# Transposing q and k of the first attention branch by VectorE and a DRAM tile, normalising x^T one section earlier, and re-timing the pre-added weight sums

## The chip, the cores and the metric

One core of a Trainium2 chip runs the whole program. The metric is the device time in microseconds of one execution; lower is better. The profiled execution that the rows come from is one such run, with its own time. Engines are named as in the profile: PE is TensorE (matmuls), DVE is VectorE, ACT is ScalarE, POOL is GpSimd, SP is SyncE, and a q behind a name is that engine's own DMA queue.

## What is computed

A decoder layer on 512 tokens of width 1024, in fp32, with two attention branches of 8 heads of 64 side by side. Cut to what matters:

```python
h = rms_norm(x, norm_w)
proj = h @ w_in
qa, ka, va, za, qb, kb, vb, zb, gl_a, gl_b = split(proj)
qa = rms_norm(split_heads(qa, 8), q_norm_w)
ka = rms_norm(split_heads(ka, 8), k_norm_w)
oa = moba_attention(qa, ka, va, rel_bias)   # at this length: causal softmax with a relative bias
ob = stick_breaking_attention(qb, kb, vb)
ya = (merge_heads(oa) * silu(za)) @ w_up_moba
yb = (merge_heads(ob) * silu(zb)) @ w_up_sb
y = sigmoid(gl_a + gb[:1024]) * ya + sigmoid(gl_b + gb[1024:]) * yb
return x + y @ w_out
```

## The kernel before

Every fp32 matmul is done as three matmuls on a high and a low part (`mm3`, lines 170 to 174): each weight chunk of 128x1024 is loaded by SP's queue as `wr` (line 124), ScalarE makes its high part `wh` (line 133) and VectorE the difference `wl` (line 135). `load_w` keeps three chunks ahead. SP, ScalarE and VectorE thus each do one step per chunk, and a chunk feeds 24 matmuls in the first part of the kernel.

Four sections come first (`section_tc`, called at lines 222, 328, 340, 347). Each computes one of qa, ka, va, vb, with tokens on the partitions, in four chunks of weights; after chunk c it calls `hooks[c]`, which is how the work on the result of the section before is put between. In the first section x^T is loaded as `xr` beside the first four weight chunks (`raw_x`, `fetch_w`) and split unnormalised. The row norms `r` are computed at the end of it (`row_norm`), and a copy `R` along the free dimension is fetched through DRAM (lines 230, 231).

qa and ka are normalised by head: ScalarE squares, VectorE sums, GpSimd makes the factors (`head_norm`), and VectorE multiplies the rows (`head_rows`, tiles `qan`, `kan`). Then TensorE transposes them, 16 blocks of 128x128 each, inside the fourth section (`head_flip`, line 313), and ScalarE and VectorE split the transposed tiles from PSUM, with the learned weight of q or k as the scale (`split`). For the fourth section and everything after it x^T is loaded once more and scaled in place by R (`normalize`, lines 234 to 240); va, the third section, still uses the unnormalised one and is scaled by r when it is split (line 343). GpSimd writes the bias table `e_sb` in 32 steps (line 337), and SP sends it to DRAM (line 339).

Then eight pairs of heads follow, four of the first branch and four of the second (lines 571 to 592). For each head: scores on TensorE, softmax or stick-breaking on ScalarE and VectorE, a transpose in 32x32 blocks on VectorE (`turn`, line 416), four DMAs to DRAM on SP's queue (`put`, line 422, tiles `pda`, `pdb`), one DMA back on ScalarE's queue (`get`, line 429, `pta`, `ptb`), and a split into `tha`/`thb` and a low part (lines 434, 435). The weighted sum with v (`weighted`, line 447) of a pair comes one pair later, so for the last pair it comes behind the loop (lines 593 to 597). Projections that nothing waits for (`FILLS`) are put between.

The last projection uses sums of blocks of `w_out`, T1 to T4, each in two halves a and b. GpSimd's queue makes each with two DMAs, the second of which adds (`sum_w`, line 103); a small copy of `turn_of` on GpSimd (line 100) holds them back until a named tile is ready: `SUMS` names the pair and head, `Y_SUMS` the output chunk. T2 is 22 + T1, T4 is 21 + T2. The chunks are used in the order of `OUT`: 11, 21, T2, T1, T3, 22, T4.

The order on each engine follows from the order in the program and from when operands are ready; `tc.issue_after` puts an instruction behind another by hand.

## Time and profile before

| | us |
|---|---|
| median of 3 runs | 401.31 (400.18 to 401.55) |
| the profiled execution, its own time | 401.33 |
| its span, first to last instruction | 399.5 |
| TensorE busy | 391.9 |
| VectorE busy | 305.3 |
| ScalarE busy | 225.1 |
| GpSimd busy | 55.6 |

The span and all times of rows are counted from the first instruction; what lies around the span is the rest of the run's time. Rows in order of time begin with the start and the length in us; behind them, in brackets, stands the idle time of the engine just before and what ended it. A granted clock of 1.00 is the full 2.4 GHz, 0.50 is 1.2 GHz.

### The profile page before, as it was taken

How to read it: one execution, taken by the hardware profiler on the slowest of the kernel's cores; microseconds unless marked ns; L12 is line 12 of the kernel's file. 1: busy time of each engine (PE TensorE's matmuls, PEld its weight loads, DVE VectorE, ACT ScalarE, POOL GpSimd, SP SyncE). 2: the span in 40 equal slices, each digit the busy share in tenths (PEclk: the TensorE clock that was granted, in tenths of full speed). 3: DMA queues.
4: the chain of work that ended last, by engine and by line, in shares of the span. 5: the costliest groups of instructions: out<-in, count | busy, mean ns of one | idle time of the engine just before them, and what ended most of it. 6: DMA issues, size and time to landing. Idle time of an engine off the chain costs nothing.

```text
span 399.5 us, 5466 instructions
## 1 busy us (share of the span) xinstructions
PE 391.9 (98%) x1884; PEld 323.5 (81%) x1884; DVE 305.3 (76%) x565; ACT 225.1 (56%) x379; POOL 55.6 (14%) x104
## 2 busy tenths in 40 slices
PE   8999999999999999999999999999999989999996
PEld 4788888888888888888888888888888868888885
DVE  4832749948888688888799599789879653999963
ACT  5782133737686969696774373373573442357540
POOL 2028964000000000000000000320020100121210
PEclk9999999999999999999999999999999998999999
DMA  7954277151667575857637717977856871479755
GB/s 262 358 224 131 80 240 260 57 159 52 172 189 237 168 233 160 255 170 210 199 94 228 219 59 215 254 215 190 254 183 153 272 209 54 157 210 258 152 149 181
DMA packets 30300, 75.12 MB, mean 188 GB/s; under 512 B 3512, under 2 KB 11960, under 8 KB 30272
## 3 DMA queue, kind: packets, MB, share of 16 engines
q1 hardware_dynamic: 23936, 52.74, 41.6%
q0 software_dynamic: 2880, 9.44, 10.6%
q10 hardware_dynamic: 3456, 12.58, 9.9%
q8 instruction: 15, 0.25, 0.3%
q14 instruction: 13, 0.11, 0.1%
HBM read 60.05 MB, written 12.61 MB: 182 GB/s over the span
## 4 chain that ended last, share of the span: by engine, by line
PE 78%; DMA 10%; DVE 5%; ACT 4%; SPq 1%; issue 1%; ACTq 0%; DVEq 0%
DMA ptb<-pdb 7%; PE gl L172 4%; PE gl L173 4%; PE gl L174 4%; PE poa L447 2%; DMA pdb<-turned 2%; PE sa L374 2%; PE za L172 2%; PE kb L172 2%; PE zb L172 2%; PE qb L172 2%; PE za L173 2%; PE kb L174 2%; PE vb L172 2%; PE qb L174 2%; PE zb L174 2%
## 5 line engine op out<-in xcount | busy, mean ns | idle before, releaser
L135 DVE TENSOR_TENSOR wl<-wr,wh 128x1024 fp32r<-128x1024 f32 (+1 forms) x63 | 76.0, 1207 | 33.6 <-ACT wh L133 29.0
L133 ACT ACTIVATE wh<-wr 128x1024 fp32r<-128x1024 f32 (+1 forms) x63 | 65.7, 1043 | 40.8 <-PE ka L174 12.2
L172 PE MATMUL gl<-xl,wh 128*128 128x512 f32 x128 | 51.4, 402 | 0.0
L173 PE MATMUL gl<-xh,wl 128*128 128x512 f32 x128 | 50.3, 393 | 0.0
L174 PE MATMUL gl<-xh,wh 128*128 128x512 f32 x128 | 50.2, 392 | 0.0
L100 POOL COPY turn_of<-thb 1x1 f32<-1x1 f32 x4 | 5.9, 1466 | 230.4 <-ACT thb L434 230.4
L174 PEld LDWEIGHTS gl<-xh,wh 128*128 128x128 f32 x128 | 24.3, 190 | 5.3
L172 PEld LDWEIGHTS gl<-xl,wh 128*128 128x128 f32 x128 | 24.3, 190 | 4.9
L173 PEld LDWEIGHTS gl<-xh,wl 128*128 128x128 f32 x128 | 24.4, 190 | 4.6
L402 DVE TENSOR_TENSOR_SCAN sx<-om,begin 128x512 f32<-128x512 f32 (+3 forms) x32 | 24.6, 807 | 0.7 <-ACT om L398 0.7
L434 ACT ACTIVATE thb<-ptb 128x1280 fp32r<-128x1280 f32 x8 | 10.2, 1270 | 22.5 <-DMA ptb<-pdb 22.5
L386 ACT ACTIVATE pa<-pa,m 128x512 f32<-128x512 f32 (+3 forms) x32 | 17.8, 559 | 6.4 <-DVE m L384 5.9
L435 DVE TENSOR_TENSOR ptb<-ptb,thb 128x1280 fp32r<-128x1280 f32 x8 | 11.9, 1489 | 11.3 <-ACT thb L434 11.3
L398 ACT ACTIVATE om<-sb 128x512 f32<-128x512 f32 (+3 forms) x32 | 14.8, 471 | 3.0 <-DVE sx L402 3.0
L416 DVE STREAM_TRANSPOSE turned<-pa 128x256 f32<-128x256 f32 (+1 forms) x48 | 15.2, 368 | 0.0
L400 ACT ACTIVATE pb<-sb 128x512 f32<-128x512 f32 (+3 forms) x32 | 15.1, 483 | 0.0
L384 DVE CUSTOM_DVE_ANT_0 pa<-sa,om 128x512 f32<-128x512 f32 (+3 forms) x32 | 14.9, 477 | 0.1
L416 DVE STREAM_TRANSPOSE turned<-pb 128x256 f32<-128x256 f32 (+1 forms) x48 | 14.7, 366 | 0.2 <-issue 0.2
L404 DVE TENSOR_TENSOR pb<-pb,sx 128x512 f32<-128x512 f32 (+3 forms) x32 | 14.2, 477 | 0.1
L435 DVE TENSOR_TENSOR pta<-pta,tha 128x1280 fp32r<-128x1280 f32 x8 | 11.8, 1474 | 2.7 <-ACT tha L434 2.7
L477 ACT ACTIVATE gl<-gl,x 128x512 f32<-128x512 f32 x16 | 11.1, 693 | 4.0 <-PE gl L174 3.9
L172 PE MATMUL kb<-xl,wh 128*128 128x512 f32 x32 | 12.7, 397 | 0.0
(322 smaller groups left out, 1064.2 us busy)
## 6 DMA issues: line engine op xcount, KB each, us to landing
wr<-in_w SPq DMA_DIRECT2D x61, 512.0 KB, 4.6
pda<-turned SPq DMA_DIRECT2D x32, 160.0 KB, 2.9
pta<-pda ACTq DMA_DIRECT2D x8, 640.0 KB, 3.9
pdb<-turned SPq DMA_DIRECT2D x32, 160.0 KB, 3.3
ptb<-pdb ACTq DMA_DIRECT2D x8, 640.0 KB, 4.6
xn<-in_x SPq DMA_DIRECT2D x8, 256.0 KB, 5.4
xs<-in_xT ACTq DMA_DIRECT2D x8, 256.0 KB, 3.0
om<-e_dr SPq DMA_DIRECT2D x8, 256.0 KB, 4.0
```

The lines of the kernel that those rows point to most:

```text
L133: A.activation(hi[:, a:b], raw[:, a:b], AF.Copy)
L135: low[c] = V.tensor_tensor(lo[:, a:b], raw[:, a:b], hi[:, a:b].bitcast(F32), op=ALU.subtract).ins
L172: T.matmul(ps, aH, bL, start=start, stop=False, skip_group_check=on)
L173: T.matmul(ps, aL, bH, start=False, stop=False, skip_group_check=on)
L174: T.matmul(ps, aH, bH, start=False, stop=stop, skip_group_check=on)
L384: V.tensor_tensor_reduce(p, sc[i], bias[:, S - n:], scale=1.0, scalar=3e38, op0=ALU.add, op1=ALU.min, accum_out=m[:, 0:1])
L386: A.activation(p, p, AF.Exp, bias=m[:, 0:1], scale=-1.0, accum_out=m[:, 1:2])
L398: A.activation(om[:, e - 1 - n:e - 1], z, AF.Sigmoid, scale=-1.0)
L400: A.activation(p, z, AF.Sigmoid)
L402: V.tensor_tensor_scan(sx[:, n - 1::-1] if n == S else sx[:, :n][:, ::-1], om[:, e - n:][:, ::-1], begin[:, S - n:][:, ::-1], 0.0, op0=ALU ...
L416: V.transpose(turned[:, :, at:at + (n - 1) * step + 1:step, :].rearrange("p q j r -> p j q r"), rows[i][:, j * P:(j + n) * P].rearrange("p ...
L435: V.tensor_tensor(pt, pt.bitcast(F32), hi.bitcast(F32), op=ALU.subtract)
```

## The change

q and k of the first branch are no longer transposed by TensorE. VectorE transposes the normalised rows in 32x32 blocks into a tile (`flip`), SP's queue writes it to a DRAM tile so that the blocks come to lie in transposed order, in runs of 512 bytes, and ScalarE's queue reads back four tiles of 128x512 (`fetch`). The split then reads SBUF (`split_flipped`); the weights of q and k are multiplied into one factor, applied to q alone. k's rows are made one chunk earlier (hook 1 of va, behind the low part of chunk 10).

x^T is loaded again in SP's queue (`reload`) during the second section and normalised in its hooks and in the first hook of the third, so that va is computed from the normalised x^T and needs no scale.

The second weight chunk is loaded and split in two halves, like the first. T1a is made one head earlier; T2b, made beside the last pair before, is made behind the first output chunk of the second branch; T3a and T3b, and T4a and T4b, are made together, the first DMAs of both ahead of the second ones.

```diff
@@ -5,7 +5,6 @@
 import concourse.bass as bass
 import concourse.tile as tile
 from concourse import mybir
-from concourse.masks import make_identity
 from concourse._compat import with_exitstack
 
 F32 = mybir.dt.float32
@@ -40,8 +39,8 @@
 BLOCKS = [b + h for b in ("11", "21", "12", "22") for h in "ab"]
 OUT = [b + h for b in ("11", "21", "T2", "T1", "T3", "22", "T4") for h in "ab"]
 
-SUMS = {(5, 0): "T1a", (5, 1): "T1b", (6, 1): "T2a", (7, 0): "T2b"}
-Y_SUMS = {1: "T3a", 3: "T3b", 5: "T4a", 7: "T4b"}
+SUMS = {(4, 1): ("T1a",), (5, 1): ("T1b",), (6, 1): ("T2a",)}
+Y_SUMS = {0: ("T2b",), 2: ("T3a", "T3b"), 5: ("T4a", "T4b")}
 
 
 FILLS = ("za:0", "za:1", "za:2", "",
@@ -94,14 +93,16 @@
     turn_of = cp.tile([1, 1], F32, name="turn_of")
     WO = w.shape[0] - len(BLOCKS)
 
-    def sum_w(name, done):
-
-        t = vp.tile([P, H // 2, 2, P], F32, tag="v", name=name).rearrange("p a b d -> p (a b d)")
+    def sum_w(names, done):
+
         with tc.issue_after(G.tensor_copy(turn_of, done[:1, :1].bitcast(F32)).ins):
-            for n, blk in enumerate(TERMS[name[:2]]):
-                src = sums[blk + name[2]] if blk[0] == "T" else w[WO + BLOCKS.index(blk + name[2])]
-                nc.gpsimd.dma_start(t, src, **({"accum_op": ALU.add} if n else {}))
-        sums[name] = t
+            for n in range(2):
+                for name in names:
+                    if n == 0:
+                        sums[name] = vp.tile([P, H // 2, 2, P], F32, tag="v", name=name).rearrange("p a b d -> p (a b d)")
+                    blk = TERMS[name[:2]][n]
+                    src = sums[blk + name[2]] if blk[0] == "T" else w[WO + BLOCKS.index(blk + name[2])]
+                    nc.gpsimd.dma_start(sums[name], src, **({"accum_op": ALU.add} if n else {}))
 
     count = [0]
 
@@ -113,13 +114,13 @@
         return ahead.pop(0)
 
     def fetch_w(c):
-        cuts = ((0, 512), (512, 1024)) if c == 0 else ((0, 1024),)
+        cuts = ((0, 512), (512, 1024)) if c < 2 else ((0, 1024),)
         if c >= WO and OUT[c - WO][0] == "T":
             raw = sums[OUT[c - WO]]
         else:
             raw = wp.tile([P, 1024], F32, tag="wr", bufs=3, name=f"wr{c}")
             for a, b in cuts:
-                if 0 < c < 4:
+                if a == 0 and 0 < c < 4:
                     raw_x(2 * c)
                 nc.sync.dma_start(raw[:, a:b], w[c if c < WO else WO + BLOCKS.index(OUT[c - WO])][:, a:b])
                 if a == 0 and c < 4:
@@ -231,16 +232,20 @@
     nc.sync.dma_start(R, bass.AP(tensor=r_dr.tensor, offset=r_dr.offset, ap=[[0, P], [1, S]]))
     Rt = R.rearrange("q (p t) -> q t p", t=NT)
 
+    again = {}
+
+    def reload(*ks):
+        for k in ks:
+            again[k] = slot(f"xs{k}")
+            nc.sync.dma_start(again[k], xT[:, SM + k * S:SM + (k + 1) * S])
+
     def normalize(k):
 
-        raw = slot(f"xs{k}")
-        nc.scalar.dma_start(raw, xT[:, SM + k * S:SM + (k + 1) * S])
+        raw = again.pop(k)
         V.scalar_tensor_tensor(blocks(raw), blocks(raw), nw[:, k:k + 1], Rt, op0=ALU.mult, op1=ALU.mult)
         A.activation(xH[k], raw, AF.Copy)
         V.tensor_tensor(xL[k], raw, xH[k].bitcast(F32), op=ALU.subtract)
 
-    ident = cp.tile([P, P], F32, name="ident")
-    make_identity(nc, ident)
     begin = cp.tile([P, S], F32, name="begin")
     G.memset(begin, 0.0)
     G.affine_select(out=begin, in_=begin, pattern=[[-1, S]], compare_op=ALU.not_equal, fill=1.0, base=S - P - 1,
@@ -297,35 +302,75 @@
             rows.append(n)
         return rows
 
-    def split(ps, name, scale, back=False):
+    def split(ps, name, scale):
 
         hi, lo = slot(f"{name}h", F32R), slot(f"{name}l", F32R)
-        h, l = (mirror(hi), mirror(lo)) if back else (blocks(hi), blocks(lo))
-        A.activation(h, blocks(ps), AF.Copy, scale=scale)
-        V.scalar_tensor_tensor(l, blocks(ps), scale, h.bitcast(F32), op0=ALU.mult, op1=ALU.subtract)
+        A.activation(hi, ps, AF.Copy, scale=scale)
+        V.scalar_tensor_tensor(lo, ps, scale, hi.bitcast(F32), op0=ALU.mult, op1=ALU.subtract)
         return hi, lo
 
-    def head_flip(rows, name, weight):
+    def flip(rows, name):
+
+        dr = dp.tile([S, S], F32, name=f"{name}dr")
+        for half in range(2):
+            tr = vp.tile([P, H // 2, 2, P], F32, tag="v", name=f"{name}t{half}")
+            tr = tr.rearrange("p a b d -> p (a b d)").rearrange("p (k i r) -> p k i r", k=8, i=NT)
+            for i in range(NT):
+                V.transpose(tr[:, :, i, :], rows[i][:, half * 256:(half + 1) * 256].rearrange("p (k c) -> p k c", k=8))
+            for a in range(4):
+                nc.sync.dma_start(bass.AP(tensor=dr.tensor, offset=dr.offset + half * 256 * S + a * P,
+                                          ap=[[S, 32], [32 * S, 8], [1, P]]),
+                                  tr[a * 32:(a + 1) * 32].rearrange("c k i r -> c k (i r)"))
+        return dr
+
+    def fetch(dr, name):
         res = []
         for p in range(H // 2):
-            pt = bank(("pj", "s")[p % 2], f"{name}T{p}")
-            for t in range(NT):
-                T.transpose(pt[:, t * P:(t + 1) * P], rows[t][:, p * P:(p + 1) * P], ident)
-            res.append(split(pt, f"{name}{p}", weight, name == "qa"))
+            res.append(slot(f"{name}T{p}"))
+            nc.scalar.dma_start(res[p], dr[p * P:(p + 1) * P, :])
         return res
 
-    nqw = cp.tile([P, 1], F32, name="nqw")
-    G.tensor_scalar(nqw, qw, -1.0, 1.0, op0=ALU.mult, op1=ALU.mult)
-    st, rows, last, qa, ka = {}, {}, {}, [], []
+    def by_block(a):
+        return a.rearrange("p i (a r) -> p i a r", a=4)
+
+    def split_flipped(raws, name):
+
+        res = []
+        for p, raw in enumerate(raws):
+            hi, lo = slot(f"{name}{p}h", F32R), slot(f"{name}{p}l", F32R)
+            src = raw.rearrange("p (a i r) -> p i a r", a=4, i=NT)
+            h, l = (by_block(blocks(x)) for x in (hi, lo))
+            if name == "qa":
+                whole = slot(f"{name}{p}")
+                A.activation(by_block(mirror(whole)), src, AF.Copy, scale=nqk)
+                src, h, l = whole, hi, lo
+            A.activation(h, src, AF.Copy)
+            V.tensor_tensor(l, src, h.bitcast(F32), op=ALU.subtract)
+            res.append((hi, lo))
+        return res
+
+    nqk = cp.tile([P, 1], F32, name="nqk")
+    G.tensor_scalar(nqk, qw, -1.0, kw, op0=ALU.mult, op1=ALU.mult)
+    st, last, qa, ka = {}, {}, [], []
 
     def norm(ps, name, scale):
         st[name] = head_norm(ps, name, scale)
 
     def spread(ps, name, c):
         with tc.issue_after(low[c]):
-            rows[name] = head_rows(ps, name, st[name])
-
-    ps_ka = section_tc(1, "ka", hooks={1: lambda: norm(ps_qa, "qa", float(HD)), 3: lambda: spread(ps_qa, "qa", 8)})
+            rows = head_rows(ps, name, st[name])
+        flipped[name] = flip(rows, name)
+
+    flipped, raws = {}, {}
+
+    def bring(name):
+        raws[name] = fetch(flipped[name], name)
+
+    reload(0, 1, 2, 3)
+    ps_ka = section_tc(1, "ka", hooks={0: lambda: norm(ps_qa, "qa", float(HD)),
+                                       1: lambda: (normalize(0), normalize(1), reload(4, 5)),
+                                       2: lambda: (normalize(2), normalize(3), reload(6, 7)),
+                                       3: lambda: (spread(ps_qa, "qa", 8), normalize(4), normalize(5))})
 
     e_dr = dp.tile([H, TW], F32, name="e_dr")
     rb = cp.tile([H, BUCKETS], F32, name="rb")
@@ -337,15 +382,13 @@
             G.tensor_scalar(e_sb[:, m:m + n], rb[:, b:b + 1].to_broadcast([H, n]), -1.0, 1.0, op0=ALU.mult,
                             op1=ALU.mult)
     nc.sync.dma_start(e_dr, e_sb)
-    ps_va = section_tc(0, "va", hooks={0: lambda: (norm(ps_ka, "ka", 1.0), normalize(0), normalize(1)),
-                                       1: lambda: (normalize(2), normalize(3)),
-                                       2: lambda: (spread(ps_ka, "ka", 11), normalize(4), normalize(5))})
-    v_of = {"a": split_v(ps_va, "va", [r[:, t:t + 1] for t in range(NT)])}
-    normalize(6)
-    normalize(7)
-
-    ps_vb = section_tc(1, "vb", hooks={1: lambda: qa.extend(head_flip(rows["qa"], "qa", nqw)),
-                                       2: lambda: ka.extend(head_flip(rows["ka"], "ka", kw))})
+    ps_va = section_tc(0, "va", hooks={0: lambda: (norm(ps_ka, "ka", 1.0), normalize(6), normalize(7), bring("qa")),
+                                       1: lambda: spread(ps_ka, "ka", 10),
+                                       2: lambda: qa.extend(split_flipped(raws["qa"], "qa"))})
+    v_of = {"a": split_v(ps_va, "va", [1.0] * NT)}
+
+    ps_vb = section_tc(1, "vb", hooks={0: lambda: bring("ka"),
+                                       1: lambda: ka.extend(split_flipped(raws["ka"], "ka"))})
     v_of["b"] = split_v(ps_vb, "vb", [1.0] * NT)
 
 
```

## Rows read from the trace of the kernel before

**Rows 1.** The page, part 1: busy us, share of span, instructions of each engine.
```profile
PE 391.9 (98%) x1884; PEld 323.5 (81%) x1884; DVE 305.3 (76%) x565; ACT 225.1 (56%) x379; POOL 55.6 (14%) x104
```

**Rows 2.** The chain that ended last, in order of time: start us, length us, what.
```profile
82.50 1.75 PE qaT L313 x16
...
129.24 1.21 PE poa L447 x8
...
254.49 0.24 PE kb L174
...
287.07 4.12 DMA ptb<-pdb
...
307.47 5.66 DMA ptb<-pdb
...
319.08 6.32 DMA ptb<-pdb
```

**Rows 3.** TensorE in order of time: start us, length us, engine, line, operation, idle before.
```profile
11.44 0.50 PE L172 MATMUL qa<-wl,xh 128*128 128x512 f32 x1 [0.43 <-DVE wl L135]
...
49.70 0.39 PE L172 MATMUL va<-wl,xh 128*128 128x512 f32 x1
...
96.86 0.50 PE L374 MATMUL sa<-ka0l,qa0h 64*128 64x512 f32 x2
...
98.20 0.80 PE L374 MATMUL sa<-ka0l,qa0h 64*128 64x256 f32 x2
...
325.23 0.39 PE L174 MATMUL gl<-xh,wh 128*128 128x512 f32 x1
...
326.80 0.85 PE L447 MATMUL pob<-thb,vbs 128*128 128x512 f32 x4 [1.18 <-ACT thb L434]
...
328.33 1.37 PE L447 MATMUL pob<-ptb,vbs 128*128 128x512 f32 x4 [0.67 <-DVE ptb L435]
...
332.02 0.40 PE L172 MATMUL gl<-xl,wh 128*128 128x512 f32 x1
```

**Rows 4.** Busy time of each engine by stretch, then granted clock, DMA share, GB/s.
```profile
48.00:58.00 10.00, 10.00 (x46) 8.29 (x45) 3.86 (x5) 1.66 (x3) 7.95 (x15) 1.00 0.62 186
330.00:332.00 2.00, 2.00 (x6) 1.56 (x5) 1.39 (x2) 0.51 (x2) 0.00 (x0) 0.54 0.64 193
```

**Rows 5.** The page, parts 5 and 6: block transposes and writes of the probabilities.
```profile
L416 DVE STREAM_TRANSPOSE turned<-pa 128x256 f32<-128x256 f32 (+1 forms) x48 | 15.2, 368 | 0.0
...
pdb<-turned SPq DMA_DIRECT2D x32, 160.0 KB, 3.3
```

**Rows 6.** VectorE in order of time, columns as in rows 3.
```profile
7.86 0.68 DVE L135 TENSOR_TENSOR wl<-wr,wh 128x512 fp32r<-128x512 f32 x1
...
10.16 1.23 DVE L135 TENSOR_TENSOR wl<-wr,wh 128x1024 fp32r<-128x1024 f32 x1 [0.80 <-ACT wh L133]
...
58.52 1.22 DVE L135 TENSOR_TENSOR wl<-wr,wh 128x1024 fp32r<-128x1024 f32 x1 [1.28 <-ACT wh L133]
...
63.80 1.88 DVE L295 TENSOR_TENSOR kan<-ka,kast 128x512 f32<-128x512 f32 x3
```

**Rows 7.** Groups by form, 28 to 97 us: busy us, mean ns, idle before.
```profile
L238 DVE SCALAR_TENSOR_TENSOR xs<-xs,x,R 128x512 f32<-128x512 f32 x8 | 9.0, 1129 | 1.9 <-DMA xs<-in_xT 1.9
```

**Rows 8.** What SP's queue waited for: us in total, times, longest.
```profile
SPq L339 <- POOL e_sb L337: 17.9, 1, 17.9
```

**Rows 9.** ScalarE in order of time, columns as in rows 3.
```profile
57.43 1.06 ACT L133 ACTIVATE wh<-wr 128x1024 fp32r<-128x1024 f32 x1 [5.09 <-DMA wr<-in_w]
...
340.69 0.42 ACT L522 ACTIVATE yh<-gl 128x256 fp32r<-128x256 f32 x1 [2.74 <-DVE gl L508]
...
366.28 1.06 ACT L133 ACTIVATE wh<-T2b 128x1024 fp32r<-128x1024 f32 x1 [0.17 <-ACT sh L522]
```

**Rows 10.** SP's and GpSimd's DMA issues in order of time, columns as in rows 3.
```profile
307.38 2.68 SPq L124 DMA_DIRECT2D wr<-in_w  x2
...
320.13 0.87 POOL L103 DMA_DIRECT2D T2b<-T1b  x1 [3.63 <-DMA T2b<-in_w]
```

## The prediction

> **What bounds the kernel now.** I read the page's busy shares first, then the chain that ended last, then TensorE in order of time wherever a row carries an idle note, then the other engines around those places. TensorE is busy for 391.9 us, 98% of the span [rows 1]. So only two things can shorten this kernel: TensorE instructions that go away, and the few places where TensorE itself waits. The reader is to see in [rows 2] that the 16 transposes of q stand on the chain as one piece of 1.75 us (the 16 of k make a second, equal piece), and in [rows 3] the two waits that matter: 0.43 us at 11.44, and 1.18 plus 0.67 us around 326.80 to 328.33, in front of the last head's weighted sum. The second costs more than its idle time, because behind it, from 330 to 332, the granted clock is 0.54, about the lower of the two levels (1.2 of 2.4 GHz) [rows 4].
>
> The matmul pitch, used below: the two sections from 49.70 to 96.86 [rows 3] hold 192 matmuls and two transpose pieces of 1.75, so (47.16 - 3.50)/192 = 0.227 us.
>
> **The transposes leave TensorE.** 2 x 1.75 = 3.50 us go, all on the chain [rows 2]. In their place VectorE gets 2 x 8 transposes of 128x256; rows of that shape take 0.368 us [rows 5], so 5.9 us on VectorE. It was busy for 3.86 of the 10 us from 48 to 58 [rows 4], so there is room, though not everywhere. The queue of SP gets 16 writes of 128 KB, that of ScalarE 8 reads of 256 KB, and ScalarE four more passes over a 128x512 tile for q. None of it is work of TensorE; it costs nothing as long as q and k are split before the first scores, and this is the cover to be worked out. k is the later one. Its normalised rows end at 63.80 + 1.88 = 65.68 [rows 6]. Eight transposes take 2.9, and two weight differences of 1.23 may stand between: 71.1 at the latest. The nearest row for the writes is that of the probabilities: 3.3 us to landing, with four of 160 KB in flight [rows 5]. Two such batches make 6.6; one batch, 3.3, is the low end, and eight in series, 26.4, the high end. I take 6.6, since the four in the row did overlap, though the runs here are shorter (512 bytes). A read of 640 KB took 4.12 to 6.32 [rows 2]; by bytes the 1 MB here takes 6.4 to 9.9, and pair 0 needs only the first quarter; I take 6.4. Adding 1.3 for a pass on ScalarE and one on VectorE (each like the 0.68 over 512 columns in [rows 6]), k is ready at 71.1 + 6.6 + 6.4 + 1.3 = 85.4. The scores would start at 96.86 - 3.50 - 0.43 = 92.9 [rows 3]: a cover of 7.5 us. With the low end it is 10.8; with the high end k is late by 12.3.
>
> A rule speaks against this edit. The Trainium skill, page VectorE: DVE Perf Modes, section Rules for kernel authors, sends a 128x128 transpose to TensorE if a PSUM destination will do, and section The three transpose paths warns that a plain DMA copy that transposes by strides is 19 times slower than the crossbar's. The trace here shows an engine without idle time on the one side and one with idle time on the other [rows 1, 4], and the strided part is done in 32x32 blocks on VectorE, so that the DMA moves whole runs; by the row the sum keeps -3.50, by the rule the slow rival below would be the likely case.
>
> **x^T normalised earlier.** The eight scalings by the row norms at 1.13 us each [rows 7], with a copy and a difference behind each, move from the third and fourth section into the second and third. VectorE's sum for them is unchanged (9.0 us for the scalings). The loads go from ScalarE's queue to SP's; SP waits there for 17.9 us for a table that GpSimd writes [rows 8], but the loads are emitted ahead of it. The third section now waits for normalised tiles: k = 0, 1 are overwritten once the second section's first chunk has been used, and are wanted at 49.70 [rows 3]. I cost this at nothing. What is late next is the weight chunk that the third section uses from its 49th matmul: ScalarE gets it at 57.43 after 5.09 us of waiting for its DMA [rows 9], VectorE ends it at 58.52 + 1.22 = 59.74 [rows 6], and TensorE wants it at 49.70 + 48 x 0.227 = 60.6. This cover is 0.9 us, or 0.4 when TensorE runs 0.43 ahead, and the new writes and reads come near it. Between nothing and one landing of writes more (3.3): I take nothing, because as many loads leave that stretch as come into it, and keep 3.3 for a rival.
>
> **Half loads of the second weight chunk.** The 0.43 us at 11.44 wait for a difference over 1024 columns of 1.23 us; over 512 it takes 0.68 [rows 6]. The first half is thus ready 0.55 earlier on VectorE alone, before counting the smaller transfer and the smaller pass on ScalarE. So the wait goes: -0.43. One more DMA issue on SP shifts the later chunks, which are not waited for. Bounds: 0 to -0.43, and I take the whole.
>
> **No half sum beside the last pair.** In [rows 3], from 325.23 to 332.02 TensorE does one pitch, eight matmuls that take 1.21 where nothing waits [rows 2], and six to seven more at the lower clock. At full clock and without the wait this is 0.23 + 1.21 + 6 x 0.227 = 2.80 instead of 6.79: 3.99 us lost, 1.85 of it idle and 2.14 at the lower clock. The wait is for the probabilities' transfer issued at 319.08, which took 6.32 [rows 2]; 1.05 us into it GpSimd issued the second half of T2b [rows 10]. With no half sum in flight the same transfer took 4.12 at 287.07, but 5.66 at 307.47 [rows 2]. At 4.12 it lands 2.20 us earlier: the high parts, 1.18 late before, come 1.0 ahead of TensorE; the low parts, 328.33 - (325.23 + 0.23 + 0.60) = 2.27 late before (0.60 is half of the 1.21), are late by 0.07. At 5.66 they are late by 1.6, and the low clock may well follow as before. I take 0.3 us left, nearer to the 4.12, because the pair at 307.47 loaded two weight chunks at that moment [rows 10]: -3.7. The sum itself moves behind the first output chunk (half split at 340.69 [rows 9]) in GpSimd's queue; it is first read at 366.28 [rows 9], 25.6 us later, while GpSimd waited 3.63 for the first of its two transfers [rows 10] and even twice that for each leaves 10 us; so it is hidden. T1a moves one head earlier, T3 and T4 start together or earlier; their readers come later still.
>
> **Sum**, against the profiled run's 401.33 (span 399.5, 1.83 around it; the median of the runs shown is 401.31, so both agree): 401.33 - 3.50 - 0.43 - 3.70 = 393.7. If nothing is left of the last wait, and the wait between the first score matmuls (0.4 us inside the 0.80 at 98.20 [rows 3]) goes too, it is 393.0; with 1.5 left, 395.2.
>
> **Rivals.**
> (a) The last pair stays late. For it: the transfer at 307.47 took 5.66 with no sum in flight [rows 2], so weight loads alone can slow it. Against: at 319.08 T2b was the one transfer beside it that the pair at 287.07 did not have. Then 1.6 us of wait stays, and with it the 2.14 of the low clock, so that 0.3 of the 3.99 is gained: 401.33 - 3.50 - 0.43 - 0.3 = 397.1.
> (b) The weight chunk of the third section comes late, because ScalarE's queue holds the reads of q ahead of it, and these wait for writes on SP. Price: 3.3 - 0.4 = 2.9 of wait and, as behind 328.33, 2.1 of low clock: 393.7 + 5.0 = 398.7.
> (c) Slower: k's way through DRAM. The writes of 512-byte runs go one after another rather than side by side, 26.4 us, and k is late by 12.3; with 2.1 of low clock this is 393.7 + 14.4 = 408.1. It decides for slower once the two together pass 8.8, that is once k is ready later than 92.9 + 6.7 = 99.6. Against it: the four writes of a head overlap in the trace. The Trainium skill's warning named above would be this case.
> (d) The change doesn't do what it says: the loop of transfer, split, stick-breaking and write that feeds the last pairs keeps its own time, and what TensorE gains is waited for at the last pair. Then all of 3.93 comes back as a longer last wait, and if T2b was not what made that wait, nothing is gained: 401. Against: the chain of waits goes from this loop back to TensorE's matmul at 254.49 [rows 2], so the loop moves with TensorE.
>
> **How the numbers follow.** The sum as worked out 0.55 (own range 393.0 to 395.2), (a) 0.18, (b) 0.13, (d) 0.06, (c) 0.08. The predicted time is the first: 393.7. Its bounds with (a) and (b) reach from 393.0 to 398.7; I put the ends at 392.8 and 398.7, which leaves out (c) and (d). About 1.2 us, 0.3%, is what a measurement here can tell from no change: faster 0.86, same 0.06, slower 0.08.
>
> **What would show it.** In the trace after, TensorE has no transposes between the fourth section's matmuls, and this section is 3.5 us shorter; the first scores follow it without a wait (otherwise (c)). The third section has no gap at its 49th matmul (otherwise (b)). The row of the last pair's transfer is 4 to 5 us long and the granted clock behind it stays at 1.00 (otherwise (a) or (d)). VectorE has 16 more transposes, all before the fourth section's end. The forecast is wrong if a new wait of TensorE over 1 us appears anywhere between 28 and 97, or if the last wait is as long as before with no half sum in flight.

## The result, and the profile after

The changed kernel takes 394.89 us (median of six runs, five of them between 393.95 and 397.16). The kernel before took 400.56 beside it (median of six, 398.12 to 401.55). Some runs, like the sixth here of 2219.94, are disturbed or in a slower state of the chip; the ratios leave these out, so that they are not always the quotient of the medians given. The ratio is 0.986, with a 95% interval of 0.982 to 0.989: 1.4% faster, clear of the noise, as forecast. 394.9 lies 1.2 above the predicted 393.7 and inside the range. In a later session the two medians were 395.43 and 400.89, ratio 0.988 (0.983 to 0.994). So the change brings some 5.5 us in these two sessions; the sum had forecast 7.6, against a profiled run that stood 0.8 above its kernel's median.

The profiled execution after took 397.16, the slowest of the five, with a span of 395.4. Its page, part 1 (busy us, share of the span, instructions), beside [rows 1]:

```profile
PE 388.7 (98%) x1852; PEld 320.6 (81%) x1852; DVE 309.7 (78%) x582; ACT 227.7 (58%) x384; POOL 56.5 (14%) x100
```

TensorE has 32 instructions fewer, the transposes, and 3.2 us less work. VectorE has 17 more and 4.4 us more. TensorE in order of time, after, at the places of [rows 3] (start us, length us, engine, line, operation, idle before):

```profile
5.64 2.04 PE L200 MATMUL qa<-wh,xh 128*128 128x512 f32 x4 [0.87 <-DVE xh L157]
...
13.17 0.39 PE L173 MATMUL qa<-wl,xh 128*128 128x512 f32 x1
...
94.86 0.50 PE L417 MATMUL sa<-ka0l,qa0h 64*128 64x512 f32 x2
...
97.01 0.35 PE L417 MATMUL sa<-ka0l,qa0h 64*128 64x256 f32 x1 [0.45 <-DVE vbs L268]
97.85 0.38 PE L417 MATMUL sa<-ka0l,qa0h 64*128 64x256 f32 x1 [0.49 <-DVE m L427]
...
324.70 0.74 PE L490 MATMUL pob<-thb,vbs 128*128 128x512 f32 x4
325.28 0.84 PE L490 MATMUL pob<-ptb,vbs 128*128 128x512 f32 x4
```

The reader is to see three things. The last pair's weighted sum (324.70) has no wait left. The matmul at 13.17 has lost its wait of 0.43, yet it starts later than its counterpart at 11.44 did. And there are two waits between the first score matmuls, 0.45 and 0.49, where [rows 3] had 0.4 in all.

To see where the time went, I cut the span of each profile at the first TensorE instruction of each product. The stretches, in us, each worked out as the difference of two starts ("again" and "both moves" are runs told of below):

| stretch | before | before again | after | after again | both moves |
|---|---|---|---|---|---|
| up to the first product | 5.29 | 5.22 | 5.64 | 5.20 | 5.52 |
| first section (qa) | 22.65 | 23.20 | 23.85 | 22.27 | 21.89 |
| second and third (ka, va) | 43.52 | 43.52 | 43.52 | 43.52 | 43.81 |
| fourth (vb) | 25.40 | 25.40 | 21.85 | 21.96 | 21.85 |
| first scores | 2.58 | 2.58 | 3.83 | 5.43 | 2.58 |
| to the second scores | 16.57 | 16.55 | 16.56 | 18.72 | 16.57 |
| to the last weighted sum but two | 195.97 | 195.97 | 195.97 | 195.98 | 196.66 |
| from there to the output chunks | 24.13 | 22.82 | 20.26 | 20.23 | 20.22 |
| output chunks, to the last matmul | 59.29 | 59.30 | 59.29 | 59.29 | 59.29 |

From before to after: -3.55 in the fourth section and -3.87 at the last pair, as the sum said; +1.20 in the first section, +0.35 in front of it and +1.25 at the first scores, which it did not say. That is -4.63 up to the last matmul; the span differs by 4.1, because the last result was written 0.5 later behind it (not followed up). Everything else agrees to a hundredth. So three places are worth an experiment, and "again" shows that all three differ between executions of one and the same kernel.

The probabilities' transfers of the second branch (tile view of `ptb`, first before, then after; issue to landing). The first view does not hold the last pair's transfer, whose 6.32 us stand in [rows 2]:

```profile
DMA to landing us min/median/max: 3.8/4.6/5.8
```

```profile
DMA to landing us min/median/max: 3.8/3.9/4.1
```

And k's way through DRAM, after: VectorE's rows and block transposes, SP's writes, ScalarE's issues of the reads, and ScalarE and VectorE behind them (columns as in [rows 3]).

```profile
70.11 2.48 DVE L300 TENSOR_TENSOR kan<-ka,kast 128x512 f32<-128x512 f32 x4
72.50 2.72 DVE L319 STREAM_TRANSPOSE kat<-kan 128x256 f32<-128x256 f32 x8
```

```profile
73.94 4.18 SPq L321 DMA_DIRECT2D kadr<-kat  x8
```

```profile
81.25 0.88 ACTq L330 DMA_DIRECT2D kaT<-kadr  x2
...
84.61 0.63 ACT L347 ACTIVATE ka0h<-kaT 128x512 fp32r<-128x512 f32 x1 [1.37 <-DMA kaT<-kadr]
85.15 1.04 ACT L134 ACTIVATE wh<-wr 128x1024 fp32r<-128x1024 f32 x1
86.10 0.62 ACT L347 ACTIVATE ka1h<-kaT 128x512 fp32r<-128x512 f32 x1
89.29 0.63 ACT L347 ACTIVATE ka2h<-kaT 128x512 fp32r<-128x512 f32 x1 [2.58 <-DMA kaT<-kadr]
90.40 0.63 ACT L347 ACTIVATE ka3h<-kaT 128x512 fp32r<-128x512 f32 x1 [0.47 <-DMA kaT<-kadr]
90.94 1.05 ACT L134 ACTIVATE wh<-wr 128x1024 fp32r<-128x1024 f32 x1
91.88 0.36 ACT L267 ACTIVATE vbs<-vb 128x256 fp32r<-128x256 f32 x1
93.61 0.66 ACT L267 ACTIVATE vbs<-vb 128x256 fp32r<-128x256 f32 x2 [1.36 <-DVE vbs L268]
```

```profile
85.28 0.69 DVE L348 TENSOR_TENSOR ka0l<-kaT,ka0h 128x512 fp32r<-128x512 f32 x1 [0.78 <-ACT ka0h L347]
```

The chain that ended last, after (start us, length us, what), at the same place:

```profile
83.44 6.93 DMA kaT<-kadr
...
97.85 0.91 PE sa L417 x10
```

k's first quarter is split by 85.28 + 0.69 = 85.97, 8.9 us ahead of the first scores. But ScalarE then stands 2.58 and 0.47 us in front of the third and fourth quarter, which nobody needs yet, and behind them in its order stand a weight chunk and the split of vb, which frees the PSUM banks that the scores write. The chain shows it: from the last read of k (landed at 90.37) it goes over a weight chunk, the split of vb on ScalarE and VectorE and a first step of the softmax to the score matmul at 97.85. Before, ScalarE had no DMA to wait for in front of that split; k's pieces came from PSUM.

### The profile page after: what moved, and what is told of

It is laid out like the page before. It is cut to its first block, busy times and chain, and to the rows that moved or that the text cites. A ratio compares the mean times of both kernels' runs of the same rounds, so it can differ in the third digit from the quotient of the medians.

```text
span 395.4 us, 5464 instructions
## 1 busy us (share of the span) xinstructions
PE 388.7 (98%) x1852; PEld 320.6 (81%) x1852; DVE 309.7 (78%) x582; ACT 227.7 (58%) x384; POOL 56.5 (14%) x100
## 4 chain that ended last, share of the span: by engine, by line
PE 79%; DVE 7%; DMA 7%; ACT 3%; issue 2%; ACTq 1%; SPq 1%; POOL 0%
PE gl L173 8%; PE gl L175 7%; PE gl L174 7%; PE pob L490 2%; PE poa L490 2%; PE sb L417 2%; PE za L173 2%; PE qa L200 2%; PE kb L173 2%; PE zb L173 2%; PE qb L173 2%; PE ya L173 2%; PE qb L175 2%; PE za L174 2%; PE ya L175 2%; PE zb L175 2%
## 5 line engine op out<-in xcount | busy, mean ns | idle before, releaser
L98 POOL COPY turn_of<-thb 1x1 f32<-1x1 f32 x3 | 3.7, 1219 | 208.2 <-ACT thb L477 208.2
L246 ACT ACTIVATE xh<-xs 128x512 fp32r<-128x512 f32 x8 | 5.0, 631 | 17.1 <-DVE xs L245 15.6
```

## The experiments

**The last pair.** Theory: the transfers of T2b, running beside the last pair's transfer, make it late. Rival: weight loads, or chance, did it.

The kernel before, with only the sums re-timed (cut to the two tables; `sum_w` is that of the changed kernel):

```diff
-SUMS = {(5, 0): "T1a", (5, 1): "T1b", (6, 1): "T2a", (7, 0): "T2b"}
-Y_SUMS = {1: "T3a", 3: "T3b", 5: "T4a", 7: "T4b"}
+SUMS = {(4, 1): ("T1a",), (5, 1): ("T1b",), (6, 1): ("T2a",)}
+Y_SUMS = {0: ("T2b",), 2: ("T3a", "T3b"), 5: ("T4a", "T4b")}
```

> The kernel before with the re-timed weight sums alone (T1a one head earlier, T2b behind the first output chunk, T3 and T4 in pairs). My theory: T2b's transfer beside the last pair's own transfer made the last wait, so without it that transfer takes about 4 us instead of 6.3, TensorE has no wait near 326 us, the granted clock there stays at 1.00, and the time is 3.7 to 4.0 us below the kernel before: a ratio of about 0.990. Rival: weight loads made the wait, or the loop of the pairs keeps its own time; then the transfer stays at 5.7 or longer, the wait stays within 0.5 us of what it was, and the ratio is 0.999 to 1.000.

Measured: 398.08 against 398.84 beside it, ratio 0.997 (0.994 to 0.999). In its profile the stretch from the last sum but two to the output chunks is 20.22, without a wait, so the mechanism is as expected. The gain in time, 0.8 by the medians and 1.3 by the ratio, is a fifth to a third of the 3.7 to 4.0 expected. Its own profile opens slowly (first section 23.97), which can't explain this, since the median holds ten runs.

The changed kernel with the old timing of the sums (cut to the two tables; `sum_w` is that of the kernel before):

```diff
-SUMS = {(4, 1): ("T1a",), (5, 1): ("T1b",), (6, 1): ("T2a",)}
-Y_SUMS = {0: ("T2b",), 2: ("T3a", "T3b"), 5: ("T4a", "T4b")}
+SUMS = {(5, 0): "T1a", (5, 1): "T1b", (6, 1): "T2a", (7, 0): "T2b"}
+Y_SUMS = {1: "T3a", 3: "T3b", 5: "T4a", 7: "T4b"}
```

> The changed kernel with the weight sums timed as before. My theory: the wait in front of the last weighted sum is back, 1.9 us of idle and a lower clock behind it, and the time is about 4 us above the changed kernel (398 to 399, a ratio of about 0.995 to the kernel before). Rival: in the changed kernel the loop of the pairs runs at another moment against the loads, so that T2b does no harm there; then it stays at 394 to 395.

Measured: 396.25 (393.82 to 398.43), ratio 0.993 (0.989 to 0.997). The wait is back in its profile, smaller (TensorE in order of time):

```profile
325.02 0.85 PE L488 MATMUL pob<-thb,vbs 128*128 128x512 f32 x4 [0.43 <-ACT thb L475]
326.55 0.85 PE L488 MATMUL pob<-ptb,vbs 128*128 128x512 f32 x4 [0.67 <-DVE ptb L476]
```

The stretch is 21.82, 1.60 more than undisturbed, with no low clock behind it. Its fastest run, 393.82, is as fast as any of the changed kernel (393.95 and 393.90 in two sessions), and a kernel of the same session with the new timing (the whole second chunk, below) took 396.15. So in some executions T2b beside the last pair seems to cost next to nothing; no profile shows one of these.

The kernel before once more, no edit:

> The kernel before itself once more. Theory 1 (the wait at the last pair, 3.99 us against an undisturbed pair, stands in every execution but its length changes): a wait of 0.5 to 4 us is there again, with the granted clock low behind it only if the wait is long. Theory 2 (it is an accident of one execution): no wait of TensorE after 320. The first section is 22.7 long as in the first profile, or about 24.3 with the slow opening.

Measured: 400.56 (one run). The wait is there again (TensorE in order of time):

```profile
327.51 0.85 PE L447 MATMUL pob<-thb,vbs 128*128 128x512 f32 x4 [1.43 <-ACT thb L434]
329.04 0.85 PE L447 MATMUL pob<-ptb,vbs 128*128 128x512 f32 x4 [0.67 <-DVE ptb L435]
```

It idles longer than in [rows 3] (1.43 + 0.67 against 1.18 + 0.67), and yet the clock stays at 1.00 behind it and the stretch is 22.82, 2.60 more than undisturbed instead of 3.91. So the low clock that I had counted at 2.14 belongs to the execution, not to the kernel.

The changed kernel with two half sums beside the last pair:

```diff
-SUMS = {(4, 1): ("T1a",), (5, 1): ("T1b",), (6, 1): ("T2a",)}
-Y_SUMS = {0: ("T2b",), 2: ("T3a", "T3b"), 5: ("T4a", "T4b")}
+SUMS = {(4, 1): ("T1a",), (5, 1): ("T1b",), (7, 0): ("T2a", "T2b")}
+Y_SUMS = {2: ("T3a", "T3b"), 5: ("T4a", "T4b")}
```

> The changed kernel with two half sums, T2a and T2b, beside the last pair, where the kernel before had one and the changed kernel has none. Theory 1 (the transfers of a half sum beside the last pair's transfer make it land late): it takes over 6 us, TensorE waits in front of the last weighted sum for 2 us or more, and the time is 2 to 4 us over the changed kernel, 397 to 399, in nearly every execution. Theory 2 (weight loads or chance alone made that transfer 6.32 us long in the profile of the kernel before): it takes 3.8 to 4.1 as in the changed kernel, and the time stays at 394.9.

Measured: 397.71 (396.25 to 404.62), ratio 0.994 (0.990 to 0.999), beside 395.43 for the changed kernel on the same chip. TensorE at the last pair, the tile view of `ptb`, and the windows behind it (length, busy time of PE, PEld, DVE, ACT, POOL, then granted clock, DMA share, GB/s):

```profile
322.94 0.86 PE L490 MATMUL pob<-thb,vbs 128*128 128x512 f32 x4 [1.16 <-ACT thb L477]
324.46 0.86 PE L490 MATMUL pob<-ptb,vbs 128*128 128x512 f32 x4 [0.67 <-DVE ptb L478]
```

```profile
DMA to landing us min/median/max: 3.7/4.1/6.4
```

```profile
325.00:328.00 3.00, 3.00 (x10) 2.43 (x9) 2.19 (x3) 1.15 (x2) 0.00 (x0) 0.54 0.48 156
328.00:331.00 3.00, 3.00 (x13) 2.37 (x13) 0.69 (x1) 0.07 (x1) 0.00 (x0) 0.89 0.13 51
```

The transfer takes 6.4 instead of at most 4.1, and the wait and the low clock (0.54) are those of [rows 3, 4], 3.95 us in all. Over the fourteen profiles of this study it is one picture: from the issue of the last transfer to ScalarE's split of it 5.65 to 6.65 us pass in the four with a half sum beside it and 3.75 to 4.09 in the ten without; the four have 1.60, 2.60, 3.91 and 3.95 us more in that stretch, the ten 0.05 at the most. The theory holds, and a half sum made beside the last pair is shown as the cause; its price changes from execution to execution.

**The transposes and the first scores.** The changed kernel with q and k transposed by TensorE again (`head_flip` and `split` as before, not shown); k's rows stay one chunk early:

```diff
-        flipped[name] = flip(rows, name)
+            rows[name] = head_rows(ps, name, st[name])
...
-                                       1: lambda: spread(ps_ka, "ka", 10),
+                                       1: lambda: spread(ps_ka, "ka", 10)})
...
-ps_vb = section_tc(1, "vb", hooks={0: lambda: bring("ka"),
-                                   1: lambda: ka.extend(split_flipped(raws["ka"], "ka"))})
+ps_vb = section_tc(1, "vb", hooks={1: lambda: qa.extend(head_flip(rows["qa"], "qa", nqw)),
+                                   2: lambda: ka.extend(head_flip(rows["ka"], "ka", kw))})
```

> The changed kernel with the 32 transposes of q and k back on TensorE; x^T normalised early, half loads and sums as in the changed kernel. My theory: 3.5 us of transposes come back on TensorE, but the longer wait at the first scores goes (they took 3.83 us from first score to the next projection in the changed kernel, 2.58 before, 2.07 for later pairs), since k's read from DRAM no longer holds ScalarE: net about 2.2 us above the changed kernel, 396.5 to 397. Rival: that longer wait has nothing to do with k's way; then it stays, and the time is 3.5 above, about 398.

Measured: 404.69 (402.46 to 405.18), ratio 1.014 (1.009 to 1.018), slower than the kernel before. The fourth section is 25.39 and the first scores are 2.59, as expected. But the third section is 29.41 instead of 21.76. Of these 7.65 us 4.93 are one wait, and behind it, from 70 to 76, the granted clock is 0.53. TensorE, then VectorE, in order of time:

```profile
70.44 0.79 PE L174 MATMUL va<-wl,xh 128*128 128x512 f32 x1 [4.93 <-DVE wl L137]
```

```profile
61.01 0.69 DVE L303 TENSOR_TENSOR kan<-ka,kast 128x512 f32<-128x512 f32 x1 [0.79 <-POOL kast L296]
63.53 0.69 DVE L303 TENSOR_TENSOR kan<-ka,kast 128x512 f32<-128x512 f32 x1 [1.83 <-POOL kast L296]
66.05 0.69 DVE L303 TENSOR_TENSOR kan<-ka,kast 128x512 f32<-128x512 f32 x1 [1.83 <-POOL kast L296]
68.57 0.69 DVE L303 TENSOR_TENSOR kan<-ka,kast 128x512 f32<-128x512 f32 x1 [1.83 <-POOL kast L296]
69.17 3.48 DVE L137 TENSOR_TENSOR wl<-wr,wh 128x1024 fp32r<-128x1024 f32 x3
```

VectorE stands four times before GpSimd's factors, and the weight differences for TensorE are queued behind. So this undoing did more than undo, and says nothing of the transposes' worth. The same again with k's rows at their old place, behind the low part of chunk 11:

```diff
-                                       1: lambda: spread(ps_ka, "ka", 10)})
+                                       2: lambda: spread(ps_ka, "ka", 11)})
```

> The changed kernel with q and k transposed by TensorE as before, k's rows made behind the low part of chunk 11 as before; the earlier normalising, the half loads and the new places of the sums stay. Theory 1 (the transposes cost 3.50 us of TensorE, of which the longer first scores give back 1.25; the 4.9 us that the former undoing waited came from k's rows one chunk earlier, standing before late factors of GpSimd): no wait of that kind, the last section 25.4 long, the first scores 2.6 long, 2.2 us over the changed kernel, some 397. Theory 2 (the early normalising delays the factors whatever the place of the rows): VectorE still stands before the factors, TensorE still waits some 5 us for a weight difference, 402 or more.

Measured: 397.95 (397.08 to 399.29), ratio 0.995 (0.992 to 0.998), between the two theories' numbers and nearer to the first. VectorE waits for GpSimd as before (1.37, 1.83, 1.83), but the two differences that TensorE needs now stand ahead of the rows, at 58.05 and 60.38, and the third section is 21.76. The fourth section is 25.40, the first scores are 2.59. Two kernels of the same session that keep the transposes off TensorE took 394.93 and 394.61 (below), so the edit is worth some 3 us; each of the two has a small edit of its own, and the changed kernel itself did not run in that session. Theory 1 stands: it was the place of the waiting rows in VectorE's order.

Why are the first scores longer after? The changed kernel with the split of k's pairs 1 to 3 put behind the split of vb:

```diff
-                                   1: lambda: ka.extend(split_flipped(raws["ka"], "ka"))})
+                                   1: lambda: ka.extend(split_flipped(raws["ka"], "ka", (0,)))})
...
+with tc.issue_after(last["vb"]):
+    ka.extend(split_flipped(raws["ka"], "ka", (1, 2, 3)))
```

> The changed kernel, with the split of k's pairs 1 to 3 put behind the split of vb in ScalarE's and VectorE's order. Theory 1 (the 3.83 us that the first scores take, against 2.58 before, come from ScalarE standing behind k's late reads, so that the split of vb and with it the banks of the scores come late): the stretch of the first scores goes back to 2.6 or less, -1.2 us, some 393.7 beside 394.9. Theory 2 (the split of vb is late for another reason, such as VectorE's own load): it stays at 3.8 and so does the time. Rival to both: k of pair 1 is then late for the second pair of scores, and a new wait of 1 us or more stands there.

Measured: 394.93 (393.53 to 396.28), ratio 0.986 (0.979 to 0.994); first scores 2.58, and no wait at the second pair. The time did not fall to the expected 393.7. The profile alone proves less than it seems, since in this execution k's reads had landed early. ScalarE in order of time shows the moved pieces:

```profile
83.24 0.64 ACT L349 ACTIVATE ka1h<-kaT 128x512 fp32r<-128x512 f32 x1 [0.20 <-DMA kaT<-kadr]
...
95.22 0.61 ACT L349 ACTIVATE ka2h<-kaT 128x512 fp32r<-128x512 f32 x1
```

More is shown by the six profiles that keep the order of the change. For each, the time from ScalarE's start on k's last quarter to the first score matmul, and the length of the first scores: 6.86 and 2.59 (two half sums), 5.52 and 2.76 (ten opening matmuls), 5.12 and 3.17 (old sums), 4.67 and 3.61 (whole second chunk), 4.46 and 3.83 (after), 3.49 and 5.43 (after again). The later k's last quarter, the longer the first scores, without exception; where it was moved out of the way they are 2.58. The split of vb, the link between the two, began 3.97, 3.97, 3.63, 3.18, 2.98 and 2.00 us ahead of the first score matmul, in the same order, and took ScalarE 5.7 to 6.0 us in all six. So its start decides, and theory 2, which had VectorE's load make it late, has at most the 0.3 us between these two. VectorE's block transposes of k ended 20.2 and 20.4 us ahead of the first score matmul in the first two profiles and 18.4 to 19.8 in the other four, so part of k's lateness stands already ahead of its way through DRAM; the slowest of its four reads, 5.6 to 7.5 us, is another part.

**The early normalising.** The changed kernel with x^T loaded on ScalarE's queue and normalised in the third and fourth section as before; va scaled when it is split:

```diff
-reload(0, 1, 2, 3)
-ps_ka = section_tc(1, "ka", hooks={0: lambda: norm(ps_qa, "qa", float(HD)),
-                                   1: lambda: (normalize(0), normalize(1), reload(4, 5)),
...
+ps_ka = section_tc(1, "ka", hooks={1: lambda: norm(ps_qa, "qa", float(HD)), 3: lambda: spread(ps_qa, "qa", 8)})
...
+                                   1: lambda: (spread(ps_ka, "ka", 10), normalize(2), normalize(3)),
+                                   2: lambda: (normalize(4), normalize(5), qa.extend(split_flipped(raws["qa"], "qa")))})
+normalize(6)
+normalize(7)
```

> The changed kernel with x^T loaded again on ScalarE's queue and normalised in the third and fourth section as before, va scaled when it is split; the transposes stay off TensorE. Theory 1 (the early normalising is free and makes nothing faster by itself; its place only stretches GpSimd's table): the table ends near 49.2 instead of 55.3, k's factors are earlier, and the time is that of the changed kernel within 0.5. Theory 2 (with k's transposes and reads in the fourth section there is no room left on VectorE and ScalarE for the normalising): TensorE waits in the third or fourth section for a normalised part or a weight difference, 2 us or more, 397 or more.

Measured: 400.32 (399.31 to 403.91), ratio 0.999 (0.995 to 1.003): without the early normalising, in this order, the rest of the change is worth nothing. The third section, counted up to the first matmul of the fourth, is 25.47 (+3.71) and the fourth 23.52 (+1.67), with a granted clock of 0.70 from 75 to 80. TensorE and VectorE in order of time:

```profile
74.90 0.80 PE L173 MATMUL vb<-wl,xh 128*128 128x512 f32 x1 [3.54 <-DVE wl L136]
```

```profile
70.39 1.13 DVE L239 SCALAR_TENSOR_TENSOR xs<-xs,x,R 128x512 f32<-128x512 f32 x1 [1.78 <-DMA xs<-in_xT]
72.58 1.12 DVE L239 SCALAR_TENSOR_TENSOR xs<-xs,x,R 128x512 f32<-128x512 f32 x1 [1.06 <-DMA xs<-in_xT]
73.62 1.22 DVE L136 TENSOR_TENSOR wl<-wr,wh 128x1024 fp32r<-128x1024 f32 x1
```

VectorE waits for a load of x^T, and the weight difference that TensorE wants stands behind. Theory 2 holds in its size; its reason, as far as the rows go, is the order on VectorE more than a lack of room; another order was not tried. Theory 1 was right about GpSimd's part alone: its last factor of k ends at 61.1 here, at 70.4 in the changed kernel.

**The second weight chunk and the opening.** The changed kernel with the second chunk loaded and split whole:

```diff
-        cuts = ((0, 512), (512, 1024)) if c < 2 else ((0, 1024),)
+        cuts = ((0, 512), (512, 1024)) if c == 0 else ((0, 1024),)
```

> The changed kernel with the second weight chunk loaded and split whole. My theory: the wait of 0.43 us ahead of that chunk's first matmul is back and nothing else: 0.4 us above the changed kernel. Rival: the slow start of the changed kernel's profiled execution (that matmul at 13.17 us, before 11.44) is made by the half loads, by one more issue on SP and two more passes ahead of other work; then it begins at 11.4 here and the time is 1 to 2 us below the changed kernel.

Measured: 396.15 (393.54 to 400.73), ratio 0.994 (0.991 to 0.997). The changed kernel did not run in that session; the interval lies above its interval in the first session and overlaps with the one in the later session, so the time decides nothing. Its first section is 23.74 and opens as slowly as that of after, so the half loads are not what made the opening slow. The wait of 0.43 did not come back in this profile: behind a slow opening it is not there with the whole chunk either. Where the opening is quick, the first section is 22.65 with the whole chunk, the wait included (one profile, [rows 3]), and 21.85 to 22.31 with the halves, without it (five profiles). The third and fourth sections are 0.40 and 0.89 longer here than after, with waits of 0.23 for VectorE's rows of k and 0.41 for a weight difference at the fourth's matmuls; this was not followed up.

The changed kernel with ten opening matmuls instead of eight:

```diff
-WARM = 8
+WARM = 10
```

> The changed kernel with ten instead of eight opening matmuls that only warm TensorE up. Theory 1 (in the executions with the longer first section of 23.85 us TensorE opens at half pitch because it has stood idle between the warm-up and the first product): the first matmuls run at full pitch in the profile, the first section is about 21.9 us, and the median falls by 1.5 to 2 us. Theory 2 (the opening pitch has nothing to do with what stood before it): the first section stays near 23.9 and the time is that of the changed kernel, or up to 0.8 us longer because the two added matmuls push the first product back.

Measured: 394.61 (393.56 to 396.93), ratio 0.987 (0.978 to 0.996). TensorE in order of time:

```profile
1.18 4.26 PE L167 MATMUL pwarm<-warm 128*128 128x512 bf16 x10 [1.18 <-DVE warm L82]
5.30 1.17 PE L200 MATMUL qa<-wh,xh 128*128 128x512 f32 x4
```

No gap, first four matmuls in 1.17 instead of 2.04, first section 21.88: the profile looks as theory 1 has it. But with eight, five of the eight profiles of kernels with half loads open as quickly too, and the median, beside 394.93 for the kernel of the session with the late split of k, did not fall by 1.5. Nor is theory 1's reason borne out: with eight, the idle time in front of the first product is 0.71 to 1.14 us in the six profiles that open quickly and 0.45 to 0.87 in the six others, so longer, if anything, where it should be shorter. What differs comes earlier, in the opening matmuls themselves (last section).

**Both moves together**, the split of k behind that of vb and ten opening matmuls, and **the changed kernel once more** (no edit) beside it:

```diff
-WARM = 8
+WARM = 10
...
-                                   1: lambda: ka.extend(split_flipped(raws["ka"], "ka"))})
+                                   1: lambda: ka.extend(split_flipped(raws["ka"], "ka", (0,)))})
...
+with tc.issue_after(last["vb"]):
+    ka.extend(split_flipped(raws["ka"], "ka", (1, 2, 3)))
```

> The changed kernel with both: k's pairs 1 to 3 split behind the split of vb, and ten opening matmuls. If both theories hold (the opening's slow pitch costs up to 2 us in some executions, k's late reads up to 1.25 in others), the profile has no wait at the first scores (2.6 long) and a first section of 21.9, and the median falls to some 393.6, with a smaller spread than that of the changed kernel beside it. If only the profile of one execution showed these, the median stays within 0.5 of the changed kernel's.

> The changed kernel itself once more, beside the others on the same chip, as the measure for them. If the first section's length and the first scores' wait change from execution to execution, this profile shows other values of them than 23.85 and 3.83, at the same instructions; if they belong to the kernel, it shows the same. The time: 394 to 395.

Measured: both moves 394.65 (394.14 to 395.73), ratio 0.986 (0.982 to 0.990); the changed kernel again 395.43 (393.90 to 398.95), ratio 0.988 (0.983 to 0.994). The profile with both moves has the 2.58 and the 21.89. The expected median of 393.6 did not come; the intervals overlap, so a gain in the median is not shown. Part of what was won is lost again in this profile: 0.29 in the second and third section, and 0.69 up to the last weighted sum but two (196.66 instead of 195.97 in the table), where a new wait of 0.4 us stands in front of a matmul of ya, for a low part of the second branch's k. The runs lie closer together (six of each). The slowest of these six runs of the changed kernel is the profiled one, and its profile explains it (TensorE, ScalarE, and the windows):

```profile
94.86 0.41 PE L417 MATMUL sa<-ka0l,qa0h 64*128 64x384 f32 x1 [0.77 <-DVE vbs L268]
96.06 0.40 PE L417 MATMUL sa<-ka0l,qa0h 64*128 64x256 f32 x1 [0.46 <-DVE vbs L268]
96.91 0.58 PE L417 MATMUL sa<-ka0l,qa0h 64*128 64x256 f32 x1 [0.44 <-DVE m L427]
```

```profile
88.80 0.63 ACT L347 ACTIVATE ka2h<-kaT 128x512 fp32r<-128x512 f32 x1 [3.06 <-DMA kaT<-kadr]
```

```profile
96.00:98.00 2.00, 1.49 (x11) 1.27 (x12) 1.87 (x5) 1.70 (x4) 0.00 (x0) 0.56 0.00 0
98.00:103.00 5.00, 5.00 (x16) 3.92 (x15) 5.00 (x22) 1.70 (x6) 0.00 (x0) 0.50 0.41 154
```

Three short waits at the first scores, and behind them the granted clock is 0.50, the lower of its two levels (1.2 GHz), for five more microseconds: 5.43 + 18.72 instead of 2.58 + 16.57, 5.0 us. This is the run of 398.95.

## Why the prediction was right, and where it was wrong

**The time** was right to 1.2 us, the sign and the range too. The gains were right in kind, but one was priced too high (the last pair), one can't be seen in the time (the half loads), and one cost was left out (the first scores). That the sum came out so near is in part luck: the two terms that change most from execution to execution, the last pair and the first scores, were a gain counted whole and a loss counted as nothing.

**Transposes off TensorE, -3.50.** The fourth section lost 3.55 in the profile, and undoing this part, with k's rows in their old place, cost some 3 us in time. The rival of the slow DRAM way (c) did not come: the reads of k were issued from 81.25 on, 3.1 us behind the last write's issue, and the first quarter was split at 85.97, against 85.4 predicted. That agreement is the sum of two errors: the block transposes ended at 75.2 instead of 71.1 (1.55 of it from the longer opening), and the way through DRAM from there took 10.8 instead of 14.3 (14.5 with the read by bytes put right: 1024 KB against the row's 640 KB make it 6.6, not 6.4). The Trainium skill, page VectorE: DVE Perf Modes, section The three transpose paths, warns of a plain DMA copy that transposes by strides where the innermost stride at the destination is large; here the blocks are turned on VectorE (2.72 us for eight) and the runs stay whole, so this case does not test the warning, and the rows show no such price.

**Its cost, taken as nothing, was the step that failed.** The prediction worked out the cover for the quarter of k that pair 0 needs, 7.5 us, and it was there (8.9). It did not ask what is queued behind the other three quarters in ScalarE's order. It is the split of vb, and through the banks it is the first scores themselves: 1.25 us in the first profile after, 5.0 with the low clock in the second, nothing where k came early. The prediction named this place only for a wait of 0.4 that might go. Of its own signs, the one that the first scores follow without a wait failed; the one of a new wait over 1 us between 28 and 97 did not come as one wait, but two of 0.45 and 0.49 in the first profile after and three that add up to 1.67 in the second do the same harm.

**Early normalising, nothing.** Right as a sum, wrong as a judgement, twice. It is no free passenger: taken out in the order that was tried, it left the change worth nothing (400.32), because VectorE waited for loads of x^T with a weight difference for TensorE behind them. And it has a price that the prediction did not see. It took k's rows to end at 65.68 as before [rows 6]; they ended at 72.6. GpSimd's table took 11.31 instead of 9.32 us, and the sums of squares of k came after the normalising on VectorE, so GpSimd waited 3.31 for them:

```profile
58.59 0.27 POOL L291 TENSOR_SCALAR kast<-kast,r2ka 128x8 f32<-128x8 f32 x1 [3.31 <-DVE kast L290]
```

Of the 6.9 us 1.55 are the longer opening; the rest makes k's last quarter later. The second profile after supports this: its opening is quick, and yet GpSimd's last factor of k ends at 70.16, against 70.37 in the first, and its first scores are the longest of all. Rival (b) did not come in the kernel as changed (the weight difference at 59.61 was done 1.3 before TensorE wanted it), but one change of order brought a wait of its kind, 4.93 us, in the same section.

**Half loads, -0.43.** The wait is gone in every profile with halves, and with a quick opening the section is 0.3 to 0.8 shorter, against one profile with the whole chunk. In the time it can't be told from nothing, because the first section changes by more than that with the opening: from 21.85 to 24.27 over the profiles with halves, from 22.27 to 23.85 between the two of the changed kernel.

**Last pair, -3.70.** The mechanism was right: no half sum beside it, transfers of 3.8 to 4.1, no wait, clock 1.00, and it comes back when a half sum is put there. The size was that of one execution. The term measured 3.9 in the first profile, 2.6 in a second one of the same kernel, 1.6 with the old sums in the changed kernel; in medians it is 0.8 in the kernel before and about 2 for two half sums in the changed one. The prediction had priced the low clock behind the wait (2.14) as if it belonged to the wait; in two of four profiles it did not follow. Rivals (a) and (d) are refuted: nothing came late again in front of the last pair.

So the sum's -3.5 - 0.4 - 3.7 became -3 to -3.5, some -0.4 that can't be told from nothing, 0 to -4 at the last pair by the execution, and a loss of 0 to 5 at the first scores that was not in it. These do not add up to one number. Two sessions gave 6.1 and 5.1 us between the medians of the runs that the ratios use. In two others the changed kernel itself did not run. There the two nearest relatives of it came out 3.1 and 2.5 us below the kernel before (whole second chunk, old sums), and 5.9 and 6.2 (late split of k, ten opening matmuls). How often each of these waits stands in an execution is not known from fourteen profiles and stays open.

## What to carry to other kernels

When a step is taken off the bounding engine and made to arrive by DMA, work out the cover not only for the part that is needed first but for every instruction that stands behind each of its waits in the order of the engine that fetches it. A wait read from one profiled execution, above all one with a low clock behind it, is priced as a range from nothing to that number until a second profile of the same kernel shows it. And undoing one part of a change can set a different trap than the part itself did: look at which instructions stand behind the moved one before reading its time as the part's worth.

## What the runs showed of the hardware that I had not expected

GpSimd's small steps on 8 partitions went several times slower while VectorE worked on two SBUF tensors. Windows of the profile after (columns as above; the fifth busy time, with its count, is GpSimd's), and VectorE in the same time:

```profile
46.00:48.00 2.00, 2.00 (x10) 1.65 (x9) 2.00 (x4) 0.94 (x2) 2.00 (x4) 1.00 0.02 4
...
50.00:52.00 2.00, 2.00 (x11) 1.65 (x10) 2.00 (x5) 1.02 (x3) 2.00 (x13) 1.00 0.00 0
```

```profile
46.05 1.29 DVE L247 TENSOR_TENSOR xl<-xs,xh 128x512 fp32r<-128x512 f32 x2
47.26 1.13 DVE L245 SCALAR_TENSOR_TENSOR xs<-xs,x,R 128x512 f32<-128x512 f32 x1
...
50.03 2.48 DVE L300 TENSOR_TENSOR qan<-qa,qast 128x512 f32<-128x512 f32 x4
```

Four steps of the table in 2 us beside the normalising, thirteen beside the rows of q, whose large operand lies in PSUM; both show GpSimd as busy throughout. The whole table took 6.50 us without the normalising beside it, 9.32 before (two scalings beside it), 11.31 after and 14.21 in the slowest case. The Trainium skill has a reason on the page SBUF — State Buffer, section SBUF: two separate sides: VectorE shares one pair of its SBUF ports with GpSimd, under an exclusive lock held for a whole instruction, and a VectorE instruction with two SBUF inputs takes it against a GpSimd instruction that reads SBUF, as the table's steps do. The trace agrees with that, four steps against thirteen, though no run here tests the lock by itself.

The opening differs between executions of the same kernel: eight opening matmuls in 3.2 to 3.5 us and then four products in 1.17, or in 3.6 and then four products in 1.65 to 2.05, with the granted clock given as 1.00 in both. Six of the twelve profiles with eight opened each way. The second costs up to 2.4 us of the first section (24.27 against 21.85). With ten, two profiles of two were quick; whether that settles it is open.
